# Pooled branch mixed by three split products, meta query products in another bank, and queries turned a group later

## The chip, the cores and the metric

The kernel runs on one core of one Trainium2 chip. The metric is the device time of one execution in microseconds (us), the median of several runs. A core has a matrix engine (TensorE, PE in the profile, with its weight loads as PEld), a vector engine (VectorE, DVE), an activation engine (ScalarE, ACT), a general one (GpSimd, POOL) and the engine that issues most of the transfers (SyncE, SP). Each runs its own list of instructions in order and waits on semaphores for the others.

## The reference

Two layers of a hybrid block work on T = 528 tokens (16 meta tokens and 512 inputs) of width 1024. In each layer the normed input h is projected; of the projection's parts these matter here:

```python
proj = jnp.einsum('btd,de->bte', h, w_in)
q = apply_rope(rms_norm(q.reshape(B, T, N_HEADS_A, HEAD_DIM), qn_g), cos_h, sin_h)
attn = indexer_sparse_attention(q, k, v, q_idx, k_idx, w_idx, k_top)   # top 128 keys of each query, by a score
...
# pooled branch: for four groups of 128 channels, running means over 2, 4, 8, 16 tokens
pooled = (jnp.concatenate(means, axis=-1) - uf)
mixed = jnp.einsum('btgc,gcd->btgd', pooled, pool_w) + pool_b
return mixed * pool_s
...
y_b = jnp.einsum('bte,ed->btd', pooled * jax.nn.silu(gate_b), w_b)
```

(The first argument of the last line is the result of the pooled branch.) Its mixing is a product of a 128x128 matrix with 528 columns for each of the four groups. Then the two branches are gated, added, projected by w_out and added to the input. All is float32.

## The kernel before, in words

**Products by parts.** Most float32 products are made of three faster ones: both operands are split into a high part (a cast to float32r, usually by ACT) and a low part (operand minus high part, usually by DVE), and high x high, high x low and low x high are added up in one PSUM bank (`dense` L588 for weight x sheet, `tok_group` L551 for token tiles). Not so the mixing of the pooled branch (`mix`, L1302): there the pooled sheet `us` and the weights `pw` go into PE as plain float32, one call for each half of the columns. Layer 0 has halves of 272 and 256 columns; layer 1 needs the last 512 columns only and takes them at once. The meta tokens' queries (`meta_queries` L545, layer 0 only) are plain float32 too: 16 short products with four stripes of the partitions side by side, which ACT copies out and one product with a folding matrix (`meta_sum`, the `fold` product, L541) adds up.

**Banks.** PSUM has eight banks under three tags: d has three (projections), a has four (mixing, turned queries, fold sums, scores), v has one. A tag's banks are taken in turn; a product that needs a bank waits until the last reader of the bank's former content is done. SBUF tags work the same way; tag C holds one large tile at a time (the index keys KI, later zb).

**Order.** The order of PE and DVE is the order in which the program issues their instructions, written out by hand; the framework places what runs on ACT and POOL. A step of work on PE is a "group" (about 3 us, one token tile or one projection half). `later(fn, n)` runs fn n groups on; `group_done` counts the groups. Between them, the steps of the top-k searches for the attention (`sel`; MAX8 and MATCH_REPLACE on DVE, tiles sc and m) are handed out by a running comparison of the PE and DVE costs issued so far (`pe_cost`, `dve_cost`, L74 and L83): the more DVE work a group has, the fewer top-k steps it gets, and these move back.

**The stretch around the change**, in each layer:

- silu of gate_b into `silb` (L1276 and on, groups j = 0 to 3); the weights `pw` are fetched (L1294).
- The pooled input u_b is projected for the groups j = 3, 2, 1, 0, two projection halves each (L1324 to L1345). POOL makes the running sums (`us`, L1340). Two to three groups later `finish` (L1298, DVE) turns sums into means less u; one group after that `mix` issues PE's products; one group later `second` (L1310, DVE, with a cast by ACT, L1315) adds the bias and multiplies by silb; one more later `third` makes the low part `mlo`.
- Meanwhile the queries run: `queries(0)`, `queries(1)` (L1268), four token tiles each; in layer 0 `meta_queries` is queued ahead of each four. A tile's product is followed by `q_post` (L656): DVE multiplies by cosine and sine tables straight from the bank (tiles t), ACT squares the same bank (L668), POOL adds, DVE makes the norms, ACT the high part and DVE the low part of `qs`, and `trans` (L693, queued at L700) has PE turn them into a bank of tag a, QN + 1 = 3 groups after `q_post`.
- The product with w_b (zb, L1370 to L1382) reads `mhi` and `mlo`.

Of the kernel before, what the change touches and what calls it, by code (L numbers as in the profile page):

```python
# [9 lines left out]
F32R = mybir.dt.float32r  # L10
AF = mybir.ActivationFunctionType
OP = mybir.AluOpType
# [5 lines left out]
T = 528  # L18
# [11 lines left out]
PB = 4  # L30
# [11 lines left out]
QN = 2  # L42
R_IDX = 3
UF = 2
QI = 3
# [46 lines left out]
def tile_block(ctx: ExitStack, tc: tile.TileContext, x, meta, w_in, pool_w, w_a, w_b, w_out, rows, hgain, c_tab, out):  # L92
    nc = tc.nc
    act, gp = nc.scalar, nc.gpsimd
    pe, dve = Metered(nc.tensor, pe_cost), Metered(nc.vector, dve_cost)

    one = ctx.enter_context(tc.tile_pool(name="one", bufs=1))
    wpool = ctx.enter_context(tc.tile_pool(name="wpool", bufs=2))
    tmp = ctx.enter_context(tc.tile_pool(name="tmp", bufs=2))
# [3 lines left out]
    def f(ap):  # L103
        return ap.bitcast(F32)
# [3 lines left out]
    def bank(tag, dt=F32):  # L108
        return psum.tile([128, 512], dt, tag=tag, name=tag, bufs=BANKS[tag])
# [234 lines left out]
    def later(fn, n=2):  # L344
        pend.append((count[0] + n, fn))

    def pump(n=1):
        for _ in range(n):
            while fill:
                try:  # L350
                    next(fill[0])
                    break
                except StopIteration:
                    fill.popleft()
# [39 lines left out]
    def drain():  # L394
        while fill:
            pump()
# [4 lines left out]
    start = one.tile([128, 2, D], F32, tag="D", name="start")  # L401
# [126 lines left out]
    def by_columns(ps, n, passes):  # L528
        for p, (h, w) in enumerate(passes):
            for k in range(KT):  # L530
                j = slice(32 * (k % 4), 32 * (k % 4) + 32)
                pe.matmul(ps[j, :n], h(k), w(k), start=p == 0 and k < 4, stop=p == len(passes) - 1 and k >= 4,
                          skip_group_check=True)
# [9 lines left out]
        later(add, 1)  # L543

    def meta_queries(g, raw):  # L545
        ps = bank("d")
        by_columns(ps, 256, [(lambda k: NM[k // 4][:, k % 4, :], lambda k: raw[k // 4][:, k % 4, :])])
        dst = qm[:, 4 * g:4 * g + 4, :]
        later(lambda: meta_sum(ps, 256, lambda total: q_post(0, total, True, dst, g)), 1)
# [51 lines left out]
    def swapped(ap, h):  # L601
        return ap.rearrange("p (h a d) -> p h a d", h=h, a=2)[:, :, ::-1, :]
# [53 lines left out]
    def q_post(t, ps, normed, dst, g=0):  # L656
        s, m = TOK[t]
        p3 = ps[:m, :256].rearrange("p (h d) -> p h d", h=4)
        t1 = tmp.tile([128, HB], F32, tag="tt", name="t1", bufs=6)
        t2 = tmp.tile([128, HB], F32, tag="tt", name="t2", bufs=6)  # L660
        v1 = t1[:m, :256].rearrange("p (h d) -> p h d", h=4)
        C, S = (Cg[:m, t], Sg[:m, t]) if normed else (ctab[:m, t], stab[:m, t])
        dve.tensor_tensor(v1, p3, C[:, None, :].to_broadcast([m, 4, 64]), op=OP.mult)
        dve.tensor_tensor(t2[:m, :256].rearrange("p (h a d) -> p h a d", h=4, a=2), swapped(ps[:m, :256], 4),
                          S.rearrange("p (a d) -> p a d", a=2)[:, None, :, :].to_broadcast([m, 4, 2, 32]), op=OP.mult)
        if normed:
            sq = tmp.tile([128, HB], F32, tag="tt", name="sq", bufs=6)
            act.activation(sq[:m, :256], ps[:m, :256], AF.Square, scale=HD ** -0.5)  # L668
            ss = small(4, "ss4")
            rq = small(4, "rq")  # L670

        def norms():
            dve.tensor_reduce(ss[:m], sq[:m, :256].rearrange("p (h d) -> p h d", h=4), axis=AX.X, op=OP.add)
            inv_rms(rq[:m] if t == 0 else RQ[:, t - 1, 4 * g:4 * g + 4], ss[:m], dve)
        if normed and t == 0:
            norms()
        added[0] = gp.tensor_tensor(t1[:m, :256], t1[:m, :256], t2[:m, :256], op=OP.add).ins  # L677
        if normed:
            qs = tmp.tile([128, 544], F32R, tag="L", name="qs", bufs=LB)[:, :512].rearrange("p (h c) -> p h c", h=4)
        else:  # L680
            qs = tmp.tile([128, 4, 128], F32R, tag="P", name="qs", bufs=PB)

        def second():
            if normed and t == 0:
                dve.tensor_tensor(v1, v1, rq[:m, :, None].to_broadcast([m, 4, 64]), op=OP.mult)
            act.copy(qs[:m, :, 0:64], v1)
            if normed and t:
                norms()

        def third():  # L690
            dve.tensor_sub(qs[:m, :, 64:128], v1, f(qs[:m, :, 0:64]))

        def trans():  # L693
            tp = bank("a", F32R)
            for h in range(4):
                pe.transpose(tp[:, h * 128:h * 128 + m], qs[:m, h, :], identr[:m, :m])
            act.copy(dst, f(tp).rearrange("p (h c) -> p h c", h=4)[:, :, :m])
        later(second, 1)
        later(third, QN if normed else QI)
        later(trans, QN + 1 if normed else QI + 1)  # L700

    SC = {}

# [514 lines left out]
    for l in range(2):  # L1218
        full = [(0, 0, HB, 0), (1, HB, T - HB, 0)]
        halves = full if l == 0 else [(1, 16, T - 16, 0)]  # L1220
# [22 lines left out]
        for what, t in (("q", 1), ("q", 2), ("k", 3), ("k", 4), ("q", 3), ("q", 4)):  # L1243
            if what == "k":
                ps = plain_group(t, raws[kv])
# [32 lines left out]
        sb = one.tile([128, 4, T], F32, tag="D", name="silb")  # L1278
        for c in range(2):
            w = chunk()  # L1280
            for mi in range(2):
                j = 2 * c + mi
                for hf, a, n, o in halves:
                    ps = dense(w, mi, a, n)
# [7 lines left out]

        pw = tmp.tile([128, 4, 128], F32, tag="B", name="pw", bufs=8)
        nc.sync.dma_start(pw, pool_w[l].rearrange("g c d -> c g d"))  # L1294
        mhi = one.tile([128, 4, T], F32R, tag="Ahi", name="mhi")
        mlo = one.tile([128, 4, T], F32R, tag="Alo", name="mlo")

        def finish(j, u, cur):  # L1298
            dve.scalar_tensor_tensor(cur[:, 16:544], cur[:, 16:544], 1.0 / (2 << j), u[:, 16:544], op0=OP.mult,
                                     op1=OP.subtract)  # L1300

        def mix(j, u, pj, l=l, pw=pw, sb=sb, mhi=mhi, mlo=mlo, halves=halves):  # L1302
            b = parT[:, 16 + 4 * l + j:17 + 4 * l + j]
            s = psc[:, 4 * l + j:4 * l + j + 1]
            pss = []
            for hf, a, n, o in halves:
                ps = bank("a")
                pe.matmul(ps[:, :n], pw[:, j, :], pj[:, 16 + a:16 + a + n], start=True, stop=True)
                pss.append(ps)

            def second():
                for (hf, a, n, o), ps in zip(halves, pss):
                    d = sb[:, j, a:a + n]
                    dve.scalar_tensor_tensor(d, ps[:, :n], b, d, op0=OP.add, op1=OP.mult)
                    act.activation(mhi[:, j, a:a + n], d, AF.Copy, scale=s)  # L1315

            def third():
                for hf, a, n, o in halves:
                    dve.scalar_tensor_tensor(mlo[:, j, a:a + n], sb[:, j, a:a + n], s, f(mhi[:, j, a:a + n]),
                                             op0=OP.mult, op1=OP.subtract)  # L1320
            later(second, 1)
            later(third, 2)

        drain()  # L1324
        for c in (1, 0):
            w = chunk()
            for mi in (1, 0):
                j = 2 * c + mi
                u = tmp.tile([128, 544], F32, tag="L", name="u", bufs=LB)
                gp.memset(u[:, 0:16], 0.0)  # L1330
                for hf, a, n, o in full:
                    ps = dense(w, mi, a, n)
                    act.copy(u[:, 16 + a:16 + a + n], ps[:, :n])
                    group_done()
                cur, other = u, None
                for e in range(j + 1):
                    d = 1 << e
                    lo_ = 2 * d - 1
                    nxt = other if other is not None else tmp.tile([128, 544], F32, tag="L", name="us", bufs=LB)
                    gp.tensor_tensor(nxt[:, lo_:544], cur[:, lo_:544], cur[:, lo_ - d:544 - d], op=OP.add)  # L1340
                    other = cur if cur is not u else None
                    cur = nxt
                gp.tensor_tensor(cur[:, 16:32], cur[:, 16:32], rect[:, j, :], op=OP.mult)
                later(lambda j=j, u=u, cur=cur: finish(j, u, cur), UF + j // 2)
                later(lambda j=j, u=u, cur=cur: mix(j, u, cur), UF + 1 + j // 2)  # L1345

        zb = one.tile([128, KT, T], F32, tag="C", name="zb")
        ta = {}
# [21 lines left out]
        for c in range(2):  # L1370
# [4 lines left out]
            for mi in range(4):  # L1375
                j = 4 * c + mi
                for hf, a, n, o in halves:
                    ps = dense(w, mi, a, n, (mhi, mlo), 4)
# [28 lines left out]
        for c in range(2):  # L1407
# [3 lines left out]
            for mi in range(4):  # L1411
                j = 4 * c + mi
                for hf, a, n, o in (halves if l == 0 else [(0, 16, HB - 16, 0), (1, HB, T - HB, 0)]):
                    ps = dense(w, mi, a, n, (ahi, alo), 4, True)
                    d = ta[j][:, a:a + n]
# [159 lines left out]
```

## Time and profile before

| | |
|---|---|
| median of 3 runs (all) | 740.64 us (740.46, 740.64, 741.62) |
| the profiled execution | 740.78 us, of which the span is 738.8 |
| granted TensorE clock | 1.00 |
| busy: PE, PEld, DVE, ACT, POOL | 731.2, 705.3, 590.0, 483.1, 246.1 us |
| layer 0: pooled projections, queries | 84 to 146 us of the span |
| layer 1: the same | 460 to 508 us |

One execution was recorded. The page gives each engine's busy time, then the span in 40 slices of 18.5 us with the busy share in tenths. The timeline lists an engine's instructions with start and duration; PE's matmuls overlap, so what one costs is the distance from its start to the next start. In brackets stands the time that an engine had nothing to do ahead of an instruction and the work that ended the wait. Of a tile's name the numbers are left out: `a<-us,pw` is a product of tiles us and pw into a bank of tag a.

### The profile page before, as it was taken

To read this page: it belongs to the slowest core of one execution; us is meant where nothing else is said; L and a number is where in the kernel's file an instruction comes from. 1 tells how busy PE (TensorE), PEld (TensorE's weight loads), DVE (VectorE), ACT (ScalarE), POOL (GpSimd) and SP (SyncE) were. 2 spreads that over 40 slices of the span, in tenths; PEclk is the share of its full clock that TensorE was granted. 3 is DMA by queue.
4 is the path that set the end of the run, shared out by engine and by line. 5 is a ranking of instruction groups with operands and counts; after the bars stand their busy time and mean duration, and the time that the engine had idled before them with its cause. 6 is when DMAs were issued, how large, how long until landed. Compare 5 with 4: busy or idle time off the path is not lost.

```text
span 738.8 us, 16099 instructions
## 1 busy us (share of the span) xinstructions
PE 731.2 (99%) x5949; PEld 705.3 (95%) x5949; DVE 590.0 (80%) x1500; ACT 483.1 (65%) x1099; POOL 246.1 (33%) x320
## 2 busy tenths in 40 slices
PE   8999999999999999999999999999999999999998
PEld 7999998899999999999999989998899999999997
DVE  6866999999997775894349668999989978768874
ACT  6769735656788886643245696367488978775643
POOL 3742173721222211163347421756031321106300
PEclk9999999999999999999999999999999999999999
DMA  8766765864564434543422678659565553439932
GB/s 266 232 171 157 165 153 115 217 157 101 134 126 114 93 81 114 173 160 116 144 89 86 171 170 201 158 125 204 114 148 110 142 115 89 116 104 266 203 88 72
DMA packets 103566, 106.41 MB, mean 144 GB/s; under 512 B 5008, under 2 KB 83632, under 8 KB 103488
## 3 DMA queue, kind: packets, MB, share of 16 engines
q1 hardware_dynamic: 91888, 74.89, 33.8%
q0 software_dynamic: 11520, 30.41, 22.9%
q8 instruction: 46, 0.75, 0.4%
q14 instruction: 32, 0.26, 0.1%
q10 hardware_dynamic: 80, 0.08, 0.1%
HBM read 66.41 MB, written 8.55 MB: 101 GB/s over the span
## 4 chain that ended last, share of the span: by engine, by line
PE 75%; DVE 17%; ACT 2%; DMA 2%; issue 2%; POOL 1%; SPq 1%; DVEq 0%; POOLq 0%; ACTq 0%
PE d L63 60%; PE a L63 10%; DVE sc L63 5%; PE v L63 4%; DVE m L63 3%; DMA xt<-in_x_dram 2%; DVE t L63 1%; DVE w L63 1%; DVE nf L63 1%; DVE silb L63 1%; DVE us L63 1%; DVE mlo L63 1%; DMA raw<-s 1%; ACT w L225 0%; SPq L156 0%
## 5 line engine op out<-in xcount | busy, mean ns | idle before, releaser
L63 PE MATMUL d<-hhi,w 128*128 128x256 f32 (+3 forms) x1392 | 278.4, 291 | 0.1
L63 PEld LDWEIGHTS d<-hhi,w 128*128 128x128 f32 x1392 | 222.2, 188 | 3.2 <-issue 0.6
L63 PE MATMUL d<-hlo,w 128*128 128x256 f32 (+3 forms) x696 | 189.8, 289 | 0.0
L63 PEld LDWEIGHTS d<-hlo,w 128*128 128x128 f32 x696 | 131.3, 189 | 1.4 <-issue 0.2
L63 DVE TENSOR_TENSOR w<-raw,w 128x512 fp32r<-128x512 f32 (+1 forms) x156 | 121.4, 784 | 13.3 <-ACT w L269 12.9
L63 PE MATMUL d<-hsum,w 128*128 128x264 f32 (+1 forms) x720 | 95.4, 285 | 0.1
L63 PEld LDWEIGHTS d<-hsum,w 128*128 128x128 f32 x720 | 89.5, 188 | 0.8 <-issue 0.3
L63 PE MATMUL d<-w,hhi 128*128 128x256 f32 x576 | 86.2, 287 | 0.7 <-ACT sq L668 0.7
L269 ACT CAST w<-raw 128x512 fp32r<-128x512 f32 x132 | 79.1, 623 | 5.6 <-DMA raw<-s 4.2
L63 PEld LDWEIGHTS d<-w,hhi 128*128 128x128 f32 x576 | 74.7, 188 | 5.2 <-issue 2.3
L255 POOL DMA_DIRECT2D raw<-raw x22 | 19.9, 903 | 114.2 <-DVE w L63 36.7
L221 POOL DMA_DIRECT2D w<-raw x34 | 31.5, 943 | 73.7 <-ACT w L220 51.1
L63 DVE MATCH_REPLACE8 sc<-m,sc 128x400 f32<-128x400 f32 (+2 forms) x100 | 54.3, 547 | 0.0
L63 DVE MAX8 m<-sc 128x8 f32<-128x400 f32 (+2 forms) x100 | 53.1, 555 | 0.9
L791 ACT ACTIVATE lt<-lt,mn,NR 128x144 f32<-128x144 f32 (+3 forms) x64 | 42.2, 661 | 12.1 <-DVE mn L63 12.0
L284 POOL DMA_DIRECT2D raw<-s x22 | 19.6, 892 | 90.6 <-DVE s L63 42.8
L63 DVE SCALAR_TENSOR_TENSOR sc<-r,wsg,sc 128x144 f32<-128x144 f32 (+3 forms) x56 | 32.4, 581 | 17.4 <-ACT r L714 15.0
L63 PE MATMUL d<-w,hlo 128*128 128x256 f32 x288 | 45.5, 281 | 0.0
L63 PE MATMUL d<-mhi,w 128*128 128x272 f32 (+2 forms) x192 | 45.3, 324 | 0.0
L806 POOL TENSOR_SCALAR pm<-lt,rs 128x16 f32<-128x16 f32 x48 | 27.9, 622 | 44.7 <-DVE rs L63 31.9
L677 POOL TENSOR_TENSOR t<-t,t 128x256 f32<-128x256 f32 (+1 forms) x34 | 32.5, 956 | 26.4 <-DVE t L63 25.0
L1420 POOL TENSOR_TENSOR hlo<-ta,hhi 128x256 fp32r<-128x256 f32 (+1 forms) x28 | 26.8, 968 | 41.5 <-PE d L63 29.4
(245 smaller groups left out, 1559.1 us busy)
## 6 DMA issues: line engine op xcount, KB each, us to landing
raw<-in_w_in_dram SPq DMA_DIRECT2D x88, 256.0 KB, 3.4
w<-raw POOLq DMA_DIRECT2D x34, 512.0 KB, 5.9
raw<-in_w_in_dram SPq DMA_DIRECT2D x32, 512.0 KB, 4.4
raw<-in_w_out_dram SPq DMA_DIRECT2D x12, 512.0 KB, 4.6
raw<-raw POOLq DMA_DIRECT2D x22, 256.0 KB, 4.0
raw<-s POOLq DMA_DIRECT2D x22, 256.0 KB, 3.7
kept<-res SPq DMA_DIRECT2D x16, 264.0 KB, 4.6
res<-kept SPq DMA_DIRECT2D x16, 264.0 KB, 6.3
```

The source lines that it names most:

```text
L63: return fn(*a, **k)
L221: gp.dma_start(t, raws[c][s], accum_op=OP.add)
L255: gp.dma_start(raws[c][0][:, 1], raws[c][0][:, 0], accum_op=OP.add)
L269: act.copy(t[:, 0], blk[src[n]])
L284: gp.dma_start(blk["a12"], blk["s2"], accum_op=OP.add)
L677: added[0] = gp.tensor_tensor(t1[:m, :256], t1[:m, :256], t2[:m, :256], op=OP.add).ins
L791: act.activation(L[hh][:, :n], L[hh][:, :n], AF.Exp, scale=NR[:, i, h:h + 1], bias=mn[:, hh:hh + 1], accum_out=sm[:, hh:hh + 1])
L806: (gp if j < 3 else dve).tensor_scalar(pms[i][:, 2 * j + hh, :], L[hh][:, 0:16], rs[:, hh:hh + 1], None, op0=OP.mult)
L1420: pool_end = gp.tensor_sub(hlo[:, j, a:a + n], d, f(hhi[:, j, a:a + n]))
```

## The change

1. **Mixing.** The weights are split into `phi` (ACT) and `plo` (DVE, a group later). `finish` also has ACT cast the pooled means to a high part and, a group later, DVE subtract it for a low part, both in the new tile `ups` (tag C, between KI and zb). `mix` is queued by `finish`, two groups after it instead of one, and issues three split products where there was one plain one.
2. **Meta queries.** The 16 short products go into v's bank instead of one of d's three.
3. **Turning.** The normed queries are turned QN + 2 = 4 groups after `q_post` instead of 3.

```diff
 def meta_queries(g, raw):
-    ps = bank("d")
+    ps = bank("v")
...
-    later(trans, QN + 1 if normed else QI + 1)
+    later(trans, QN + 2 if normed else QI + 1)
...
+    phi = tmp.tile([128, 4, 128], F32R, tag="P", name="phi", bufs=PB)
+    plo = tmp.tile([128, 4, 128], F32R, tag="P", name="plo", bufs=PB)
+
+    def split_pw(pw=pw, phi=phi, plo=plo):
+        act.copy(phi, pw)
+        later(lambda: dve.tensor_sub(plo, pw, f(phi)), 1)
...
-    def finish(j, u, cur):
-        dve.scalar_tensor_tensor(cur[:, 16:544], cur[:, 16:544], 1.0 / (2 << j), u[:, 16:544], op0=OP.mult,
-                                 op1=OP.subtract)
+    def finish(j, u, cur, halves=halves):
+        a = halves[0][1]
+        c = cur[:, 16 + a:544]
+        dve.scalar_tensor_tensor(c, c, 1.0 / (2 << j), u[:, 16 + a:544], op0=OP.mult, op1=OP.subtract)
+        if not ups:
+            ups.append(one.tile([128, 4, 2, T], F32R, tag="C", name="ups"))
+        hi, lo = ups[0][:, j, 0], ups[0][:, j, 1]
+        act.copy(hi[:, a:], c)
+        later(lambda: dve.tensor_sub(lo[:, a:], c, f(hi[:, a:])), 1)
+        later(lambda: mix(j, hi, lo), 2)
...
         for hf, a, n, o in halves:
             ps = bank("a")
-            pe.matmul(ps[:, :n], pw[:, j, :], pj[:, 16 + a:16 + a + n], start=True, stop=True)
+            for e, (p, x_) in enumerate(((phi, hi), (plo, hi), (phi, lo))):
+                pe.matmul(ps[:, :n], p[:, j, :], x_[:, a:a + n], start=e == 0, stop=e == 2)
...
     drain()
+    split_pw()
...
             later(lambda j=j, u=u, cur=cur: finish(j, u, cur), UF + j // 2)
-            later(lambda j=j, u=u, cur=cur: mix(j, u, cur), UF + 1 + j // 2)
```

More of the change, by code (lines that the diff above doesn't have):

```diff
@@ L1294, in tile_block, with mix @@
         nc.sync.dma_start(pw, pool_w[l].rearrange("g c d -> c g d"))
+        phi = tmp.tile([128, 4, 128], F32R, tag="P", name="phi", bufs=PB)
[3 more added lines that the diff above has]
+            later(lambda: dve.tensor_sub(plo, pw, f(phi)), 1)
         mhi = one.tile([128, 4, T], F32R, tag="Ahi", name="mhi")
         mlo = one.tile([128, 4, T], F32R, tag="Alo", name="mlo")
-        def finish(j, u, cur):
-            dve.scalar_tensor_tensor(cur[:, 16:544], cur[:, 16:544], 1.0 / (2 << j), u[:, 16:544], op0=OP.mult,
-                                     op1=OP.subtract)
-        def mix(j, u, pj, l=l, pw=pw, sb=sb, mhi=mhi, mlo=mlo, halves=halves):
+        def finish(j, u, cur, halves=halves):
[8 more added lines that the diff above has]
+            later(lambda: mix(j, hi, lo), 2)
+        ups = []
+        def mix(j, hi, lo, l=l, phi=phi, plo=plo, sb=sb, mhi=mhi, mlo=mlo, halves=halves):
             b = parT[:, 16 + 4 * l + j:17 + 4 * l + j]
```

## The prediction

> **What bounds the kernel now.** First the page: busy shares, the slices, the chain, and the group of ACT casts that the new casts resemble.
>
> ```profile
> PE 731.2 (99%) x5949; PEld 705.3 (95%) x5949; DVE 590.0 (80%) x1500; ACT 483.1 (65%) x1099; POOL 246.1 (33%) x320
> ...
> DVE  6866999999997775894349668999989978768874
> ...
> PEclk9999999999999999999999999999999999999999
> ...
> PE 75%; DVE 17%; ACT 2%; DMA 2%; issue 2%; POOL 1%; SPq 1%; DVEq 0%; POOLq 0%; ACTq 0%
> ...
> L269 ACT CAST w<-raw 128x512 fp32r<-128x512 f32 x132 | 79.1, 623 | 5.6 <-DMA raw<-s 4.2
> ```
>
> PE is busy 99% of the span at an unchanged clock, so PE time taken out is time won, unless a new wait eats it. DVE averages 80%, but the slices show runs of nines: there DVE has no slack. Next, PE's waits (total, times, longest) and the stretches that hold the change: layer 0's and layer 1's two query groups, with the pooled branch's mixing (busy us of PE, PEld, DVE, ACT, POOL).
>
> ```profile
> PE d L63 <- DVE ss L63: 1.5, 1, 1.5
> PE d L63 <- ACT sq L668: 0.7, 1, 0.7
> PE a L63 <- DVE qs L63: 0.6, 1, 0.6
> ```
>
> ```profile
> 106.00:131.00 25.00, 24.31 (x202) 21.63 (x200) 24.22 (x63) 12.27 (x24) 11.48 (x17) 1.00 0.43 95
> 131.00:146.00 15.00, 15.00 (x125) 14.34 (x126) 14.33 (x43) 10.06 (x21) 10.11 (x13) 1.00 0.94 246
> ...
> 473.00:495.00 22.00, 22.00 (x168) 20.08 (x167) 21.73 (x54) 8.76 (x16) 10.45 (x14) 1.00 0.67 164
> 495.00:508.00 13.00, 12.40 (x109) 12.22 (x108) 12.86 (x37) 9.83 (x18) 8.04 (x11) 1.00 0.78 172
> ```
>
> The 1.5 is at the start of the kernel. The other two waits lie in these stretches and are what the bank and the later turning aim at. But DVE is idle only 0.78 us of 25 and 0.27 of 22 there: PE and DVE are both full, and whatever the change adds to DVE in front of something that PE needs comes out as a PE wait.
>
> **The change part by part.** PE in layer 0, from its timeline (start, duration):
>
> ```profile
> 106.13 1.05 PE L63 MATMUL a<-us,pw 128*128 128x272 f32 x4
> ...
> 107.15 0.29 PE L63 MATMUL d<-hlo,w 128*128 128x272 f32 x1
> 107.28 0.29 PE L63 MATMUL d<-hhi,w 128*128 128x272 f32 x1
> ...
> 114.85 1.21 PE L63 MATMUL d<-w,hhi 128*128 128x256 f32 x8
> ...
> 117.79 1.05 PE L63 MATMUL a<-us,pw 128*128 128x272 f32 x4
> ...
> 121.61 0.60 PE L63 MATMUL a<-part,fold 128*16 128x256 f32 x2
> ...
> 131.00 1.22 PE L63 MATMUL d<-w,hhi 128*128 128x256 f32 x8 [0.69 <-ACT sq L668]
> ```
>
> and in layer 1:
>
> ```profile
> 473.59 1.02 PE L63 MATMUL a<-us,pw 128*128 128x512 f32 x2
> ...
> 474.58 0.29 PE L63 MATMUL d<-hlo,w 128*128 128x272 f32 x1
> ...
> 494.09 0.45 PE L63 MATMUL a<-identr,qs 128*128 128x128 f32 x4
> ...
> 501.25 0.50 PE L63 MATMUL a<-identr,qs 128*128 128x128 f32 x4 [0.60 <-DVE qs L63]
> ...
> 508.31 0.39 PE L63 MATMUL d<-mlo,w 128*128 128x512 f32 x1
> 508.54 0.40 PE L63 MATMUL d<-mhi,w 128*128 128x512 f32 x1
> ```
>
> *Mixing on PE.* A split product of 272 columns costs 0.125 us from start to start (107.15 to 107.28). One mixing step runs from 106.13 to one such product before 107.15: 0.89 us for 528 columns in plain float32. Three split products cost 3 x (0.125 + 0.12, the 256 columns in proportion) = 0.73. Four steps: 0.63 us won. In layer 1 the step takes 473.59 to 474.455 = 0.87; a 512-column product takes 0.235 (508.31 to 508.54), three take 0.71: 4 x 0.16 = 0.62 won. **PE: -1.25 us.**
>
> *Bank and turning.* With the meta products in v's bank, the first product at 131.00 finds a d bank that was read long before: its 0.69 us goes, about 0.75 with the refill. Turned a group (some 3 us) later, the queries of 501.25 are ready: its 0.60 goes, also some 0.75. **-1.5 us.** Nothing is added by either; DMAs and the queues of SP and POOL keep their order, apart from waits on DVE below.
>
> *The splits.* Per layer ACT gets five casts (row above: 0.62 us each; ACT works 12.27 of 25 us there, so they hide), and DVE gets five subtractions, one for the weights and one per group j. They delay DVE. Its timeline in layer 0:
>
> ```profile
> 93.91 1.32 DVE L63 TENSOR_TENSOR hsum<-nf,hsum 128x528 fp32r<-128x528 f32 x2
> 95.15 0.09 DVE L63 MATCH_VALUE_LOAD sc<-m,sc 128x8 f32 x1
> ...
> 117.72 0.87 DVE L63 SCALAR_TENSOR_TENSOR silb<-a,parT,silb 128x272 f32<-128x272 f32 x2
> ...
> 120.39 1.17 DVE L63 MAX8 m<-sc 128x8 f32<-128x400 f32 x2
> 121.49 0.88 DVE L63 SCALAR_TENSOR_TENSOR mlo<-silb,psc,mhi 128x272 fp32r<-128x272 f32 x2
> 122.28 0.70 DVE L63 SCALAR_TENSOR_TENSOR us<-us,u 128x528 f32<-128x528 f32 x1
> 122.90 0.89 DVE L63 SCALAR_TENSOR_TENSOR silb<-a,parT,silb 128x272 f32<-128x272 f32 x2
> 123.70 0.40 DVE L63 TENSOR_TENSOR t<-a,Cg 16x256 f32<-16x256 f32 x1
> ...
> 127.44 1.21 DVE L63 TENSOR_TENSOR qs<-t,qs 128x256 fp32r<-128x256 f32 x1
> 128.57 0.41 DVE L63 TENSOR_TENSOR t<-t,rq 16x256 f32<-16x256 f32 x1
> ```
>
> Two 528-wide subtractions take 93.91 to 95.15, so one takes 0.62. The gating addition of one group (`silb`, L1310, two halves) takes 0.80 (122.90 to 123.70), `mlo` 0.79, the pair of MAX8 1.10 (120.39 to 121.49), of which the 528-wide one 0.6 by width.
>
> The hand order of the changed kernel puts the gating addition of group 2 behind the finishing of group 0 (`us` at 122.28), because mixing comes a group later. Between hsum and that `us`, DVE gets the weights' subtraction and those of groups 3, 2, 1 (4 x 0.62 = 2.48) and loses `silb` and `mlo` of group 2 and one 528-wide MAX8, which now come after it (0.80 + 0.79 + 0.6 = 2.2). So `us` starts at 122.28 + 0.28 = 122.55 and the first half of silb(2) is done at 122.55 + 0.62 + 0.4 = 123.55, where the whole of it was done at 118.5 before.
>
> Who waits for it: tag a has four banks. Mixing of groups 2 and 1 fills four; the sum of the meta query (the `fold` product, 121.61) needs the next one, that of group 2's first half. PE reaches it at 121.61 less three steps' 0.16 = 121.15. **New wait: 123.55 - 121.15 = 2.4 us**, and the projections of two query tiles stand behind it in PE's order. I bound it by 1.3 (no DVE instruction slowed by POOL work beside it) and 3.2.
>
> Then group 0. Before, DVE took 123.70 to 128.57 = 4.87 us for the meta tile's rotation, its sums, one rotation, one `mlo`, one `qs`. After the fold product at 123.55 it starts at about 124.2, with one MAX8 (0.6) and silb(1) (0.8) more ahead of group 0's subtraction: that ends at 124.2 + 4.87 + 1.4 + 0.62 = 131.1, or 0.8 earlier, at 130.3, if `qs` takes 0.41 instead of the 1.21 of the row. PE wants it at 123.55 + 0.54 (fold) + 2 x 2.94 (114.85 to 117.79 is one query tile) + 0.25 (its first two products need only the high part) = 130.2. **Wait 0.1 to 0.9, I take 0.4.** Layer 0: -0.63 - 0.75 + 2.4 + 0.4 = **+1.4**.
>
> Layer 1 has no meta queries and one bank per step, so no fold. There the last subtraction counts:
>
> ```profile
> 492.45 0.96 DVE L63 TENSOR_TENSOR qs<-t,qs 128x256 fp32r<-128x256 f32 x1
> 493.33 0.41 DVE L63 TENSOR_REDUCE ss<-sq 128x4 f32<-128x256 f32 x1
> ```
>
> By 493.33 DVE has done what will stand ahead of group 0's subtraction, except four subtractions to come (4 x 0.6), and less one `mlo` (0.66) and one 528-wide MAX8 (0.6) that come later: it starts at 494.45 and ends at 495.05, or 494.5 if `qs` isn't slowed. PE would have the step, now behind the third query tile, at 494.09 - 0.62 - 0.71 = 492.75, and needs the low part 0.47 later, at 493.2. **Wait 1.3 to 1.8, I take 1.5.** Layer 1: -0.62 - 0.75 + 1.5 = **+0.1**.
>
> The steps of the two late top-k searches (MAX8, MATCH_REPLACE) are pushed back by what DVE is given, about one round. The attention that uses them shows DVE at 5 to 8 tenths (slices 12 to 15 and 32 to 35), so I cost this at nothing; a round is 2.3 us (two pairs), and if half of one came out on the path it would cost about 1.
>
> Sum: 740.78 (the profiled execution, its span of 738.8 and 1.98 around it) + 1.4 + 0.1 = **742.3 us**. The median, 740.64, lies 0.14 below that execution, so this is 0.2% over the median: the edge of what a measurement of this kernel tells from no change (0.2%, 1.5 us).
>
> **Where a page speaks against the change.** A DVE operation beside POOL work has this range (minimum, median, maximum ns):
>
> ```profile
> L63 DVE SCALAR_TENSOR_TENSOR us<-us,u x8: 687/694/1011, 104.2 to 489.3; 128x528 f32<-128x528 f32 x8
> ```
>
> `us` is stretched by 0.32 once in eight, `qs` by 0.8 at 127.44. The Trainium skill (SBUF — State Buffer, "Who interferes with whom") says that a VectorE operation with two SBUF inputs and a GpSimd operation that reads SBUF block one another for a whole instruction; the new subtractions have two such inputs. By that rule any of them can meet POOL's prefix sums; the rows agree that some two-input operations are stretched, and most are not.
>
> **The rivals.**
> *A, the waits don't come.* It decides at silb(2): if DVE is through with it by 121.15, 2.4 us earlier than I sum, and with group 0's by 130.2 and 493.2, all of the PE gain stays: 740.78 - 1.25 - 1.5 = **738.0**. For it: some of DVE's time is stretching beside POOL, which another order may avoid. Against: DVE has 0.78 us of idle in 25, the order is fixed, and the bank's reader is fixed. Faster by 0.4%. Chance 0.22.
> *B, half.* The stretched operations fall away in both layers (-1.1 at the fold, -0.4 at group 0, -0.4 in layer 1): 742.3 - 1.9 = **740.4**, no difference. Chance 0.14.
> *C, the subtractions are stretched.* By 0.3 (the `us` row) to 0.8 (`qs`), four in each layer ahead of what PE waits for: 4 x 2 x 0.3 = 2.4 more, **744.7**, slower; it decides by whether POOL's additions run beside them (POOL is busy 11.48 of 25 us). Chance 0.14.
>
> **How the numbers follow.** The forecast has 0.50, with a range of its own of 740.9 to 743.9 (fold 1.3 to 3.2, the rest by its bounds); 0.2 of that lies within 0.2% of the median, 0.3 above. Faster: A, 0.22. Same: 0.20 + 0.14 = 0.34. Slower: 0.30 + 0.14 = 0.44. The range takes in A and C: 737.8 to 744.9.
>
> **What the profile after would show.** Right: the mixing groups at 0.73 and 0.71 us; PE's waits with `fold` behind DVE `silb` (some 2.4) and `a` products behind the low part (0.4 and 1.5); none behind sq L668 at 131 or qs at 501; DVE without idle from 95 to 131. Wrong: a fold product without a wait (then A or B), `us` of group 0 well before 122, a wait at the first product of the next projection (banks of d held by late rotations, which I cost at nothing with a margin of under 1 us), or top-k steps on the chain in the attention.

## The result and the profile after

| | before | after |
|---|---|---|
| median of 6 runs each, us | 741.13 | 752.19 |
| ratio, 95% interval | | 1.0149, 1.0135 to 1.0163 |
| span of the profiled execution, us | 738.8 | 749.8 |

The change makes the kernel 1.5% slower, 11 us. The prediction said 742.3, with a range of 737.8 to 744.9.

First the page of the changed kernel, busy time and DVE's slices:

```profile
PE 734.2 (98%) x5961; PEld 708.3 (94%) x5961; DVE 596.9 (80%) x1510; ACT 488.5 (65%) x1109; POOL 245.5 (33%) x320
...
DVE  6876999998898775794449667999989988768874
```

PE's busy time did not fall (matmul records overlap, so its 734.2 is no sum of costs, and part of it ran at a lower clock, see below); DVE has ten more instructions and 6.9 us more. PE's waits, as quoted of before (total, times, longest):

```profile
PE a L63 <- DVE silb L63: 2.3, 1, 2.3
PE a L63 <- ACT r L714: 1.9, 1, 1.9
PE d L63 <- ACT sq L668: 1.7, 2, 1.0
PE d L63 <- DVE ss L63: 1.5, 1, 1.5
PE a L63 <- DMA xt<-in_x_dram: 1.1, 1, 1.1
PE a L63 <- DVE ups L63: 1.1, 1, 1.1
PE d L63 <- DVE w L63: 1.0, 2, 0.8
```

The start's 1.5 is as before; the transfer of x (1.1) is at the start too and moves by about this much from execution to execution. The others are new: 8.0 us (two of less than 0.5 are left out). Where they lie, from PE's timeline in layer 0:

```profile
109.96 0.29 PE L63 MATMUL a<-ups,phi 128*128 128x272 f32 x1
...
110.69 0.28 PE L63 MATMUL d<-hhi,w 128*128 128x256 f32 x1
...
124.32 0.59 PE L63 MATMUL a<-part,fold 128*16 128x256 f32 x2 [2.30 <-DVE silb L63]
...
132.11 0.52 PE L63 MATMUL a<-ups,phi 128*128 128x272 f32 x2 [1.08 <-DVE ups L63]
...
148.68 0.39 PE L63 MATMUL d<-mhi,w 128*128 128x272 f32 x1 [0.66 <-ACT sq L668]
...
151.50 0.39 PE L63 MATMUL d<-mhi,w 128*128 128x256 f32 x1 [1.04 <-ACT sq L668]
```

A mixing step takes 109.96 to 110.69 = 0.73 us, as summed. Then come four waits: the fold, group 0's low part, and two at the first halves of the product with w_b, whose d banks are still read by late rotations. In layer 1 the first loss lies ahead of the pooled branch. ACT's timeline, then PE's:

```profile
455.36 0.62 ACT L1299 CAST phi<-pw 128x512 fp32r<-128x512 f32 x1 [4.05 <-DMA pw<-in_pool_w_dram]
```

```profile
463.40 0.50 PE L63 MATMUL a<-KI,qi 128*128 128x256 f32 x2 [1.89 <-ACT r L714]
```

The new cast of the pooled weights stands in ACT's queue ahead of the activations of the index scores (`r`, L714) and waits 4.05 us for a transfer; PE's score products behind it need the banks that `r` would empty. Right after that wait the granted clock fell. These are the windows of the changed kernel in which it did and the one behind it (busy PE, PEld, DVE, ACT, POOL, then the clock):

```profile
463.93:467.34 3.41, 3.41 (x12) 2.88 (x11) 3.17 (x9) 2.83 (x7) 0.99 (x2) 0.50 0.78 154
467.34:470.00 2.66, 2.66 (x23) 2.66 (x23) 2.52 (x8) 1.61 (x3) 0.00 (x0) 1.00 0.83 184
```

For 3.4 us PE ran at half its clock: 272-column products start every 0.225 us there (466.34 to 466.56) and every 0.125 us behind it.

The same product in both timelines, start after less start before, tells where the 11 us arise:

| landmark (start before, us) | shift, us | so the stretch cost |
|---|---|---|
| first projection after the start, 59.8 | +0.7 | 0.7, x's transfer |
| first product of layer 0's attention, 171.6 | +5.5 | 4.7, pooled branch and queries of layer 0 |
| index scores of layer 1, 449.5 | +6.4 | 0.9, mostly layer 0's attention |
| pooled projections of layer 1, 470.1 | +10.6 | 4.3: 2.8 from the held cast, then 1.5 from the half clock |
| first product of layer 1's attention, 533.2 | +9.4 | -1.3, queries of layer 1 |
| last product, 735.0 | +10.9 | 1.6, behind |

The half clock was not in this execution alone: the mean granted clock was 0.993 to 0.999 in the six of the changed kernel, 0.993 in the slowest (754.42 us), and 0.998 to 1.000 in those of the kernel before. By my estimate 3.4 us at half clock in 750 lower the mean by 0.002. Not every wait is followed by it: after the fold's 2.30 us the clock stayed at 1.00 here, and what decides is not shown.

### The profile page after: what moved, and what is told of

Its sections match the earlier page's. It is cut to its first block, busy times and chain, and to the rows that moved or that the text cites. A ratio compares the mean times of both kernels' runs of the same rounds, so it can differ in the third digit from the quotient of the medians.

```text
span 749.8 us, 16141 instructions
## 1 busy us (share of the span) xinstructions
PE 734.2 (98%) x5961; PEld 708.3 (94%) x5961; DVE 596.9 (80%) x1510; ACT 488.5 (65%) x1109; POOL 245.5 (33%) x320
## 4 chain that ended last, share of the span: by engine, by line
PE 65%; DVE 19%; DMA 5%; ACT 4%; issue 3%; POOL 2%; SPq 1%; DVEq 0%; POOLq 0%; ACTq 0%
PE d L63 52%; PE a L63 9%; DVE sc L63 5%; PE v L63 4%; DVE m L63 3%; DVE t L63 2%; DMA xt<-in_x_dram 2%; DVE w L63 2%; DVE nf L63 1%; DMA raw<-in_w_in_dram 1%; DVE silb L63 1%; ACT w L220 1%; DMA pw<-in_pool_w_dram 1%; POOL t L677 1%; DVE mlo L63 1%
## 5 line engine op out<-in xcount | busy, mean ns | idle before, releaser
L63 PE MATMUL d<-w,hhi 128*128 128x256 f32 x576 | 84.4, 284 | 0.0
```

Of the source, the lines that this page charges most:

```text
L63: return fn(*a, **k)
```

## The experiments

Two theories for the 11 us, and their rivals; neither counts the clock. **Held cast**: about 4 us are ACT's wait for the pooled weights; rival: the casts' and subtractions' work itself. **DVE paces**: the rest is DVE's added work in stretches where it had no room; rivals: mixing a group later with its bank (the fold), or the two small edits. Each ratio is to the kernel before, run on the same chip.

### bank_turn: the two small edits alone

```diff
 def meta_queries(g, raw):
-    ps = bank("d")
+    ps = bank("v")
...
-    later(trans, QN + 1 if normed else QI + 1)
+    later(trans, QN + 2 if normed else QI + 1)
```

> The kernel before with the meta products in v's bank and the queries turned a group later; the mixing stays one plain product. Theory 'two stalls': both waits at 131 (0.69) and 501 (0.60) go and nothing else moves, 739.2 to 739.6, ratio 0.998. Rival 'the turning is what costs later': the turning products only move into the next stretch and the change's loss is partly here, 741 to 743.

Measured: 741.38 against 740.44 us, ratio 1.0008 (0.9995 to 1.0021). The two waits are gone, and the time is not less. The median lies in the rival's range, but the interval takes in no change, so a loss isn't shown either. PE's timeline shows where the gain went:

```profile
145.29 0.39 PE L63 MATMUL d<-mhi,w 128*128 128x256 f32 x1 [0.23 <-ACT sq L668]
...
534.71 4.33 PE L63 MATMUL d<-hsum,w 128*128 128x256 f32 x34 [0.90 <-DVE w L63]
...
554.04 0.51 PE L63 MATMUL d<-hhi,w 128*128 128x256 f32 x2 [0.25 <-DVE w L63]
```

At 533 PE is 1.6 us earlier than before, and DVE's subtraction for the weights of 534 only 0.4 (533.97 against 534.38). At 145 PE waits for banks that DVE and ACT still read; at 534 and 554 for weights that DVE splits. By the last product PE stands 0.16 ahead of before, less than the 0.6 by which this execution was already ahead before either edit came.

### bank_only: the bank alone

```diff
 def meta_queries(g, raw):
-    ps = bank("d")
+    ps = bank("v")
```

> The kernel before with only the meta products in v's bank. Theory 'given back': the 0.7 at 131 goes, but DVE's rotations are no earlier and the banks of d are waited for at the product with w_b instead: 740 to 741, ratio 0.999 to 1.001. Rival 'it was the turning that gave it back in bank_turn': the 0.75 stays, 739.6 to 739.9, ratio 0.999.

Measured: 741.68 against 740.60, ratio 1.001 (0.9998 to 1.0022). The median is 0.7 above the expected range, and the interval takes in no change. Given back, as expected: 0.78 won by the first product of the second queries, 0.21 left at layer 0's attention.

### mix_only: the splits without the two edits

```diff
 def meta_queries(g, raw):
-    ps = bank("v")
+    ps = bank("d")
...
-    later(trans, QN + 2 if normed else QI + 1)
+    later(trans, QN + 1 if normed else QI + 1)
```

(against the changed kernel)

> The changed kernel with only the three split products (meta products in a bank of d, queries turned after 3 groups). Theory 'the loss is all in the splits': 752.2 plus the 1.5 that the other two parts win, 753 to 754. Rival 'the parts work against one another': the fold or the later turning makes part of the waits, 749 to 751.

Measured: 752.73 against 740.44, ratio 1.0162 (1.0141 to 1.0182). That is 0.3 below the expected range. The loss is in the splits; the two edits change it by no more than the intervals. (In the recorded execution the clock fell to 0.50 for 3.4 us twice, at 125.6 behind the fold's wait and at 463.5 behind the held cast.)

### cast_only: one cast by ACT, and nothing else

```diff
 drain()
+idp = tmp.tile([128, 4, 128], F32R, tag="P", name="idp", bufs=PB)
+act.copy(idp, pw)
```

(against the kernel before)

> The kernel before with one more ACT cast per layer, that of the pooled weights, its result unused. Theory 'held cast': ACT waits some 4 us for the transfer in layer 1 ahead of the index scores' activations: 4.3 of shift by the pooled projections, 1 to 2 of it made up behind: 742.5 to 745. Rival 'the cast is hidden': 740.4 to 741.

Measured: 743.89 against 741.38, ratio 1.0034 (1.0020 to 1.0049), 2.5 us, as the theory had it; in the profiled execution 3.7 of span. ACT's timeline of this kernel:

```profile
449.51 0.62 ACT L1326 CAST idp<-pw 128x512 fp32r<-128x512 f32 x1 [4.57 <-DMA pw<-in_pool_w_dram]
```

A 0.62 us instruction costs 2.5 to 3.7 us by its place. The clock stayed at 1.00 here, and the hold cost 3.3 us of shift between 449.5 and 470.1. The fetch is issued at 443 (SP's rows of before) behind a weight transfer, and lands 6.0 us later; nothing but the mixing at 473 needed it before.

### cast_early: the same cast, and the fetch earlier

```diff
+pw = tmp.tile([128, 4, 128], F32, tag="B", name="pw", bufs=8)
+nc.sync.dma_start(pw, pool_w[l].rearrange("g c d -> c g d"))
 kept = dram.tile([128, KT, T], F32, name=f"kept{l}")
...
-pw = tmp.tile([128, 4, 128], F32, tag="B", name="pw", bufs=8)
-nc.sync.dma_start(pw, pool_w[l].rearrange("g c d -> c g d"))
```

(against cast_only)

> As cast_only (the kernel before and one unused cast of the pooled weights by ACT per layer), with the fetch of these weights issued ahead of the second half of the index queries. Theory 'held cast': the transfer is done when the cast's turn comes, ACT does not wait, and the 3.6 us of shift of cast_only go: 740.3 to 741.3. Rival 'the cast itself or its buffer': 743 to 745 as cast_only.

Measured: 741.16 against 740.78, ratio 1.0002 (0.9993 to 1.0011). The cast's rows in this kernel (minimum, median, maximum ns, first and last start):

```profile
L1326 ACT CAST idp<-pw x2: 641/646/652, 61.7 to 430.0; 128x512 fp32r<-128x512 f32 x2
```

No wait is listed for it, and its loss is gone: the wait for the transfer was the cause, not the cast or its buffer.

### early_load: the changed kernel with the fetch earlier

The edit is that of cast_early, made in the changed kernel.

> The changed kernel with the fetch of the pooled weights issued ahead of the second half of the index queries, some 20 us earlier. Theory 'held cast': ACT's cast of these weights stands in front of the index scores' activations and waits 4.05 us for the transfer in layer 1; with the transfer done, the 4.3 us of shift at 455 to 468 go, of which 1 to 2 come back as a wait for group 0's low part (DVE caught up during the hold): 748 to 749.5. Rival 'more work': the shift comes from ACT's and DVE's added work or the order of transfers, 751.5 to 752.5.

Measured: 749.97 against 740.44, ratio 1.0124 (1.0107 to 1.0140), 0.5 above the forecast range. The hold is gone: PE's shift against before is 6.1 us both at 449.5 and at 470.1. On the same chip mix_only and fold_v, which keep the hold, took 752.73 and 753.51; beside the changed kernel's own ratio of 1.0149 the intervals overlap a little. Part of the gain comes back. PE's waits in layer 1's pooled branch and queries, 470 to 520 us, where the changed kernel has none:

```profile
PE a L63 <- DVE ups L63: 2.2, 2, 1.3
```

The theory had this wait, and took it that ACT's hold had let DVE catch up in the changed kernel. The rows show something else as well. PE waits 1.34 of it at 484.67, behind this subtraction:

```profile
483.11 1.50 DVE L63 TENSOR_TENSOR ups<-us,ups 128x512 fp32r<-128x512 f32 x1
```

It took 0.68 in the changed kernel; here POOL's additions run beside it. And fold_v (next), which keeps the hold, has the stretched subtraction (1.50 at 487.16) and waits too, from 470 to 520 us:

```profile
PE a L63 <- DVE ups L63: 2.4, 2, 1.6
```

So the hold alone doesn't explain why the changed kernel had no such wait. Its PE also ran at half clock behind the hold, which gave DVE another 1.5 us; mix_only, where the clock fell there too, has no wait for `ups` either. Which of the two mattered, and how far the stretching by itself, is not separated.

### fold_v: the fold in v's bank

```diff
-def meta_sum(ps, n, then):
+def meta_sum(ps, n, then, tag="a"):
...
-        total = bank("a")
+        total = bank(tag)
...
-    later(lambda: meta_sum(ps, 256, lambda total: q_post(0, total, True, dst, g)), 1)
+    later(lambda: meta_sum(ps, 256, lambda total: q_post(0, total, True, dst, g), "v"), 1)
```

(against the changed kernel)

> The changed kernel with the sum of the meta queries in v's bank instead of one of a. Theory 'bank': the wait of 2.30 at the fold goes and the two query tiles behind it start earlier; DVE has the same work, so the wait for group 0's low part grows from 1.1 to 2 or so: 749.5 to 751.2. Rival 'DVE paces this stretch': all of it comes back at group 0 and at the next product with w_b, 751.7 to 752.4.

Measured: 753.51 against 740.44, ratio 1.0168 (1.0151 to 1.0185): above both ranges, and no gain; that it is slower than the changed kernel isn't shown, the intervals overlap. PE's waits from 95 to 177 us:

```profile
PE a L63 <- DVE ups L63: 2.9, 1, 2.9
PE d L63 <- ACT sq L668: 1.7, 2, 1.1
```

The fold's 2.3 is gone, group 0's wait grew from 1.1 to 2.9, and the 1.7 at w_b stands. In layer 0 the bank mostly chose where PE waits for DVE. The recorded execution then ran at clock 0.50 from 131.5 to 134.9, behind the wait of 2.9.

### five_subs: DVE's added work, and nothing else

```diff
 def finish(j, u, cur):
     dve.scalar_tensor_tensor(...)
+    later(lambda: idle_sub(cur, u), 1)      # dve.tensor_sub of cur and u into an unused tile
...
 drain()
+idp = tmp.tile([128, 4, 128], F32R, tag="P", name="idp", bufs=PB)
+later(lambda pw=pw, idp=idp: dve.tensor_sub(idp, pw, pw), 1)
```

(against the kernel before; the mixing stays one plain product, a group after `finish`)

> The kernel before, its mixing untouched, with five subtractions of the same size added on DVE in each layer where the change has them (one beside the weights, one a group after each finish), their results unused. Theory 'DVE paces the stretch': 3 us of DVE work per layer come out as waits of PE, in part later when DVE hands on what it was late with: 744 to 747. Rival 'the splits' work is hidden, what costs is mixing a group later and its bank': 740.5 to 741.5.

Measured: 751.22 against 741.38, ratio 1.0136 (1.0112 to 1.0161): 10 us, more than either theory gave, from ten subtractions. They took 7.8 us: nine of them 0.67 to 0.70 each, and one, beside POOL's additions, 1.58:

```profile
468.56 1.58 DVE L63 TENSOR_TENSOR idp<-pw 128x512 fp32r<-128x512 f32 x1
```

Windows from the end of hsum to the start of layer 0's attention (busy PE, PEld, DVE), of before, of this kernel and of the changed one:

```profile
95.00:171.60 76.60, 75.91 (x629) 72.42 (x628) 74.47 (x200) 42.12 (x86) 39.65 (x48) 1.00 0.64 152
```

```profile
95.00:176.20 81.20, 77.80 (x627) 73.71 (x627) 76.89 (x203) 41.88 (x86) 40.77 (x48) 0.98 0.61 143
```

```profile
95.50:177.10 81.60, 76.52 (x641) 73.02 (x640) 77.49 (x203) 45.08 (x91) 40.53 (x48) 1.00 0.62 143
```

Before, DVE is idle 2.1 us of 76.6 and PE 0.7. With five subtractions both are idle longer: DVE 4.3, PE 3.4 (5.1 in the changed kernel). The stretch grows by 4.6 us although the added work is 3.5 and about one round of the late top-k moved behind it (13 instead of 14 of its MAX8). PE's waits in it:

```profile
PE a L63 <- DVE qs L63: 1.2, 1, 1.2
PE d L63 <- ACT sq L668: 1.1, 2, 1.0
PE d L63 <- ACT zb L1390: 1.1, 1, 1.1
```

They are other waits than in the changed kernel. But waits are not all. PE's busy time grew by 1.9 us with the same work, and the row above has a clock of 0.98. It fell as the wait of 0.95 for `sq` ended (132.39):

```profile
132.17:135.58 3.41, 3.19 (x15) 3.19 (x16) 3.38 (x11) 3.02 (x7) 3.41 (x5) 0.50 0.98 190
```

PE's shift against before grows by 1.4 us across it (from 1.4 at 131.0 to 2.8 at 132.8). Without it the stretch grew by 3.2 to 3.4, about the 3.5 of added work. In layer 1, from 470 to 533, the shift grows by 4.0, for 4.3 of added work at a clock of 1.00; between the layers by 0.8. So in this run added DVE work came out at about its length where both engines are full, and the clock came on top. One thing besides work is in this edit: the subtraction reads the buffer of `u` a group later, and POOL waits for that twice, 2.9 us in all, which the changed kernel does not have.

### pool_lows: the low parts on POOL

```diff
-    later(lambda: dve.tensor_sub(plo, pw, f(phi)), 1)
+    gp.tensor_sub(plo, pw, f(phi))
...
-    later(lambda: dve.tensor_sub(lo[:, a:], c, f(hi[:, a:])), 1)
+    gp.tensor_sub(lo[:, a:], c, f(hi[:, a:]))
```

(against early_load)

> The changed kernel with the early fetch, and all low parts of the pooled mixing subtracted by POOL instead of DVE. Theory 'DVE paces': DVE has its work of before again; what stays is the wait of the fold, since mixing is still a group later (about 2): 742 to 744.5. Rival 'POOL is late': its additions of 1.1 us and the new subtractions delay one another and the mixing waits for low parts, 747 to 750.

Measured: 749.43 against 741.38, ratio 1.0108 (1.0090 to 1.0127), where early_load had 1.0124: no gain that the intervals show. The number lies in the rival's range, but PE waits for no low part in this run; it waits 2.8 for the fold (with a clock of 0.50 behind it, 124.3 to 127.7) and 2.5 for the banks of d. DVE has 1500 instructions again, as before, but its busy time on the page stays as in early_load (598.0 with 1510):

```profile
PE 732.8 (98%) x5961; PEld 707.5 (95%) x5961; DVE 597.7 (80%) x1500; ACT 487.9 (65%) x1109; POOL 258.9 (35%) x330
```

Its groups by shape from 95 to 172 us (busy us, mean ns), first of before, then of this kernel:

```profile
L63 DVE TENSOR_TENSOR qs<-t,qs 16x256 fp32r<-16x256 f32 x2 | 1.2, 604 | 0.0
...
L63 DVE SCALAR_TENSOR_TENSOR silb<-a,parT,silb 128x272 f32<-128x272 f32 x4 | 1.9, 486 | 0.0
L63 DVE SCALAR_TENSOR_TENSOR mlo<-silb,psc,mhi 128x272 fp32r<-128x272 f32 x4 | 1.9, 482 | 0.0
```

```profile
L63 DVE SCALAR_TENSOR_TENSOR mlo<-silb,psc,mhi 128x272 fp32r<-128x272 f32 x4 | 3.5, 874 | 0.0
...
L63 DVE TENSOR_TENSOR qs<-t,qs 16x256 fp32r<-16x256 f32 x2 | 2.4, 1182 | 0.0
...
L63 DVE SCALAR_TENSOR_TENSOR silb<-a,parT,silb 128x272 f32<-128x272 f32 x4 | 2.0, 488 | 0.0
```

`mlo` and `qs`, which read two SBUF tiles, take on average almost twice their time; `silb`, which reads a PSUM bank and one SBUF tile, takes what it took. The means hide that single instructions are stretched: of the four pairs of `mlo` halves one took 2.47 us (at 117.97, POOL being busy beside it) and the others 0.88 to 0.89, as before; in early_load one took 1.79. The Trainium skill (SBUF — State Buffer, "Who interferes with whom") has the rule that a VectorE operation with two SBUF inputs contends with a GpSimd operation that reads SBUF; the rows agree. What DVE saved, it paid back in stretching.

### pool_lows_fold_v: the same with the fold in v's bank

The edit is that of fold_v, made in pool_lows.

> As pool_lows, and the sum of the meta queries in v's bank. Theory 'DVE paces': the fold's wait goes and DVE has room to use it, unlike in fold_v: 739.5 to 742, at or below the kernel before. Rival 'POOL is late': no better than pool_lows, 746 to 750.

Measured: 747.71 against 741.38, ratio 1.0086 (1.0066 to 1.0105): 1.7 us below pool_lows, and still 6 above before; the rival's range. The bank is worth a little, and far from what this theory had expected. The fold's wait is gone, and PE waits 4.4 us for the banks of d instead of 2.5.

### short_before and short_after: room on DVE

```diff
 def topk_steps(tiles):
-    for rnd in range(16):
+    for rnd in range(6):
```

(the first against the kernel before, the second against early_load)

> The kernel before with six of the sixteen rounds of each top-k search (ten rounds left out, so fewer keys are chosen): DVE has room from about the first query tiles on. Theory 'DVE paces': the two waits of 0.7 and 0.6 go or shrink and little else, since PE was already 99% busy: 737.5 to 740. Rival 'PE alone sets it': 740 to 741.

> The changed kernel with the early fetch (early_load) and the same six rounds. Theory 'DVE paces': with room on DVE the waits for low parts, for the fold and at the product with w_b shrink to little, and the 1.25 of PE show: within 1.5 of short_before, 737 to 741, where early_load was 9 above before. Rival 'order and banks': mixing a group later and the fold's bank cost the same whatever DVE has to do, 745 to 749.

Measured on one chip: 739.98 and 741.91 against 740.60; ratios 0.9989 (0.9980 to 0.9998) and 1.0017 (1.0008 to 1.0026). short_before came out as forecast; short_after misses its range by 0.9 and its distance by 0.4, and is far from the rival's. Between early_load and before lay 9.5 us; with room on DVE, 1.9 are left. PE's waits of short_after from 95 to 177 us:

```profile
PE a L63 <- DVE silb L63: 1.0, 1, 1.0
PE a L63 <- DVE ups L63: 0.6, 1, 0.6
```

The waits at w_b are gone and the other two are about half. Before 131 us DVE still is full here (23.77 of 25 us from 106 to 131, by the windows of this run). One more wait is left, in layer 1, from 470 to 520 us:

```profile
PE a L63 <- DVE ups L63: 1.4, 1, 1.4
```

It stands behind a subtraction that took 1.56 us, stretched as in early_load (at 478.06, with one of POOL's additions beside it). So about four fifths of the loss without the hold is DVE's lack of room, and mixing by split products did not win even where DVE had more of it.

## Why the prediction was wrong

- **Mixing on PE, -1.25: right.** 0.73 in layer 0; in layer 1 the next rows give 0.70.

```profile
493.60 0.40 PE L63 MATMUL a<-ups,phi 128*128 128x512 f32 x1
...
494.30 1.10 PE L63 MATMUL d<-w,hhi 128*128 128x256 f32 x8
```

- **The fold's wait, 2.4: right in place and size** (2.30 behind silb(2), which starts at 123.68, or 122.94 less the 0.74 by which this execution starts later; the sum had 122.55 + 0.62 = 123.17). As a cause it fails: fold_v took it away, and the time stayed.
- **Group 0 in layer 0, 0.1 to 0.9: 1.08, a little beyond.** DVE's rows show why:

```profile
123.68 0.89 DVE L63 SCALAR_TENSOR_TENSOR silb<-a,parT,silb 128x272 f32<-128x272 f32 x2
...
128.51 1.80 DVE L63 SCALAR_TENSOR_TENSOR mlo<-silb,psc,mhi 128x272 fp32r<-128x272 f32 x2
...
131.37 0.69 DVE L63 TENSOR_TENSOR ups<-us,ups 128x528 fp32r<-128x528 f32 x1
```

  The pair of `mlo`, stretched beside POOL, took 1.80 instead of 0.87 to 0.89. The `qs` that the sum had stretched by 0.8 took 0.41 (at 130.2): the size is right partly by luck.
- **"Per layer ACT gets five casts (row above: 0.62 us each; ACT works 12.27 of 25 us there, so they hide)": the step that failed most, 4.3 us of shift.** The cast of the weights does not stand in that stretch but where the framework puts it, ahead of the index scores in ACT's queue, and waits there for a fetch that had come in time for its old reader only. I counted ACT's work and not what the cast waits for, nor who is queued behind it. cast_only and cast_early show it, early_load in the changed kernel. The hold alone is worth 3.0 to 3.3 us (fold_v, cast_only, clock 1.00 behind it), the rest is the clock.
- **"At an unchanged clock": failed too, about 1.5 us.** I took the clock of before for the changed kernel's. It fell to 0.50 for 3.4 us behind a wait, in the recorded execution behind ACT's hold.
- **"I cost at nothing with a margin of under 1 us", the d banks at the product with w_b: 1.7 us in layer 0.** **The late top-k "at nothing"**: 0.9 us arise between the two layers' stretches, with a new wait of 0.4 for `c`; that it is the moved rounds was not tested by itself.
- **Bank and turning, -1.5: the waits went, the gain did not stay** (bank_turn, 1.0008). The sum took a wait away and did not ask what PE, now earlier, would find late next: the same DVE.
- **Layer 1, +0.1: the wait of 1.3 to 1.8 was absent in the changed kernel.** It is 2.2 without the hold (early_load), but also 2.4 with it where the clock stayed up (fold_v). That layer 1's queries won 1.3 us, as the two gains alone would give, was luck of the hold and the clock before them.
- **Rivals.** A and B did not happen. Nor did C in the recorded execution of the changed kernel: the low parts' subtractions took 0.675 to 0.704 us all eight times, and DVE's busy time rose by the ten subtractions' own sum (6.9 us). In early_load, fold_v and short_after two of the ten were stretched, to about 1.5 us each, so C's mechanism is real in this kernel, though it isn't the cause of these 11 us. (C's row of `us` has two long ones of eight, 1.01 and 0.96, and not one.)

As a whole: I added up single waits along one path, at an unchanged clock. Three things were missing: a queue held by a late transfer, DVE work that comes out in full wherever DVE is full, and the clock behind a wait. In layer 0 the changed kernel lost 4.7 us, after mixing had won 0.6, with 3.5 of DVE work and no fall of the clock there; five_subs with the same work lost 3.2 to 3.4 without the clock's part. The difference, of 1 to 2 us, is not taken apart: the stretched `mlo`, mixing a group later and its bank are all in it.

## What to carry to other kernels

When two engines are both 97% busy in a stretch, price work that you shift onto either of them at its full length; a saving on one of them alone isn't kept (0.73 for 0.89 us on PE, against 0.69 us on DVE and one cast, was a bad trade). Read the clock of each stretch in every run beside the waits. For each new instruction ask what its inputs wait for and which instructions stand behind it in its engine's queue: a 0.62 us cast cost 2.5 us because its transfer was late. Read a wait that vanishes as an order for the next one: look up what is late next before you book the gain.

## What the hardware showed that was not expected

Moving a subtraction from DVE to POOL did not unload DVE: POOL took 1.28 to 1.34 us for a low part that takes DVE 0.69, and some of DVE's own two-tile operations beside it were stretched (a pair of `mlo` from 0.89 to 2.47 us), so that DVE's busy time was 597.7 us with 1500 instructions, against 590.0 with the same number before.

The granted clock fell to 0.50 for 3.41 us in the middle of five of the fourteen recorded executions, in mix_only twice, each time within 1.5 us of the end of a wait of PE of 0.95 to 2.93 us. It cost 1.4 us more in five_subs and 1.5 in the changed kernel. After other waits as long (2.30 at the changed kernel's fold, 1.89 in cast_only) it stayed at 1.00. That the wait brings it down is inferred from these places, not tested.
